# Inverse key norms written out on POOL and spread by whole transposes, and one slot more for mixed inputs, in a four-layer encoder trunk

## The chip, the core and the metric

The kernel runs on one core of a Trainium2 chip. The core has a TensorE (PE, with its weight loads shown apart as PEld), a VectorE (DVE), a ScalarE (ACT), a GpSimd (POOL) and a SyncE (SP) that issues transfers; all run their own instruction queues in order and meet through semaphores. The metric is the device time of one execution in microseconds (us), as the median of several.

## The reference

A sequence of 512 positions with 1024 channels passes two pairs of sub-layers, in fp32: a chunked spatial-gating MLP, a gated feed-forward with a short convolution, an RWKV-7 time mixer, a second such feed-forward, and a last RMS norm. The change touches the time mixer alone. What matters of it:

```
xx = token_shift(h) - h
xk = h + xx * mu[2];  xv = h + xx * mu[3]      # likewise xr, xw, xa, xg
k = xk @ w_k;  v = xv @ w_v                    # likewise r, the decay w, a, g
kk = heads(k * k_k)                            # 16 heads of 64 channels
kk = kk * rsqrt(max(sum(kk * kk, -1), 1e-24))  # a norm per position and head
k = k * (1 + (a - 1) * k_a)
y = wkv7_scan(r, exp(-exp(w)), k, v, -kk, kk * a)
```

The scan updates a 64 x 64 state per head at each position; `-kk` and `kk * a` are the two vectors of its rank-one correction.

## The kernel before

Activations are held transposed: 128 channels on the partitions, 512 positions along the free axis, in eight tiles. Every dense matmul is made of three (`mm3`, L325 to L327): high part of the weight by high part of the input, high by low, and low by high, each 128x128 by 128x512. An input tile therefore exists twice, as `mxh` and `mxl`, in a ring of ten slots for each of the two tags. `mix(i, k)` makes one: ScalarE scales the shifted tile (L669), VectorE adds the unshifted one (L670), ScalarE rounds the high part (L237), VectorE subtracts for the low part (L238).

The time mixer has three stages. First the low-rank inputs and r are projected. Then the *pairs* stage works through the eight pairs of heads (one tile of 128 channels is one pair): `decay`, `operands` and `products` make from the projected keys what the scan needs, per chunk of 64 positions, and write it to DRAM. At the same time the projections of k and v (`projections`) run as *fill*: the generator `weave` asks the fill for some steps of dense matmuls after every step of the pairs. Then the two groups of four pairs are scanned chunk by chunk, with the inversion of small triangular blocks (`invert`), the gate and the output projection beside it. The instructions are emitted in this woven order, and a scheduling layer then orders each engine's queue; the queues are in order on the chip.

In `decay`, of pair p: two matmuls (L875, L877) give decay and a, ScalarE takes their tanh, VectorE scans the decay within chunks (L887), and ScalarE makes three exponentials of it (L892, L893, L895). For the norm, ScalarE squares the scaled key (`sq`, L889), four matmuls of 2 columns (L899) sum the squares of each head, with the result turned so that positions lie on partitions: 8 numbers on each of 128 partitions (4 blocks of 128 positions, 2 heads). VectorE bounds them (L901) and takes the reciprocal (L902), `n2`. These have to be spread back over the 64 channels of each head: eight matmuls (L907), one for each block and head, whose weights are one column of `n2` repeated 64 times and whose moving operand is the identity; the result `u.q` lies in PSUM.

`operands` multiplies the scaled key by it (L926) and makes the operand tiles `ar` (L920, L921) and `bk` (L927, L928, L930, copy L933). `products` multiplies `bk` by `ar` (L949) and by a diagonal (L963) and masks the results (L953). The large scratch tile with the tag `sq` exists twice, and a pair uses it twice: for the tanh of the decay (`th`, in which the scan result lies too) and for the squares.

The keys' projection takes m = 0 to 5 one by one (each eight input tiles) and the last two together, k by k. In that last loop the values' inputs `xv` are made, up to three ahead (`k + 3`): with ten slots, eight are the keys' inputs.

## Time and profile before

| | |
|---|---|
| median of 3 runs | 1257.34 us (1256.7 to 1258.81) |
| the profiled execution, its own time | 1258.93 us |
| its span, first to last instruction | 1257.1 us |
| mean granted TensorE clock in it | 0.994 |
| busy PE / DVE / ACT / POOL | 1240.7 / 857.7 / 628.1 / 95.0 us |
| the eight groups of L907 | from 583.3 to 687.8 us |

A row of a timeline has the start and the length in us, the engine, line, operation, what is written and read, the shape, and how many instructions were merged. A group row has the busy time, then the mean length in ns, then the idle time before it and what ended that. A released wait names the engine and the line that were waited for. Matmuls are pipelined, so a row's length reaches past the start of the next; the distance of two starts is what an instruction takes of the engine. A matmul of two fp32 passes shows as two records, a transpose as one.

### The profile page before, as it was taken

To read this page: it belongs to the slowest core of one execution; us is meant where nothing else is said; L and a number is where in the kernel's file an instruction comes from. 1 tells how busy PE (TensorE), PEld (TensorE's weight loads), DVE (VectorE), ACT (ScalarE), POOL (GpSimd) and SP (SyncE) were. 2 spreads that over 40 slices of the span, in tenths; PEclk is the share of its full clock that TensorE was granted. 3 is DMA by queue.
4 is the path that set the end of the run, shared out by engine and by line. 5 is a ranking of instruction groups with operands and counts; after the bars stand their busy time and mean duration, and the time that the engine had idled before them with its cause. 6 is when DMAs were issued, how large, how long until landed. Compare 5 with 4: busy or idle time off the path is not lost.

```text
span 1257.1 us, 19429 instructions
## 1 busy us (share of the span) xinstructions
PE 1240.7 (99%) x7543; PEld 1005.7 (80%) x7543; DVE 857.7 (68%) x1413; ACT 628.1 (50%) x1081; POOL 95.0 (8%) x116
## 2 busy tenths in 40 slices
PE   9999999999999999999999999899999999999997
PEld 6878888888888888877777777678888888888886
DVE  6466568888886445675889888675677777772323
ACT  5534445555554433475677657433545444442322
POOL 4100200000000001000000013222100000000000
PEclk9999999999999999999999989999999999999999
DMA  7332357777656776325878887654323333233332
GB/s 250 113 101 84 107 174 247 246 241 248 205 172 193 225 227 195 95 92 186 216 196 230 223 270 224 224 152 135 98 88 100 101 101 90 95 97 95 107 93 80
DMA packets 125133, 201.65 MB, mean 160 GB/s; under 512 B 39856, under 2 KB 63152, under 8 KB 125040
## 3 DMA queue, kind: packets, MB, share of 16 engines
q10 hardware_dynamic: 38976, 112.87, 29.3%
q1 hardware_dynamic: 86064, 87.54, 22.4%
q8 instruction: 59, 0.97, 0.3%
q14 instruction: 34, 0.28, 0.1%
HBM read 152.93 MB, written 47.45 MB: 159 GB/s over the span
## 4 chain that ended last, share of the span: by engine, by line
PE 88%; DVE 5%; issue 1%; ACT 0%; DMA 0%; POOL 0%; ACTq 0%; DVEq 0%; POOLq 0%
PE mm L325 9%; PE mm L326 9%; PE mm L327 9%; PE aux L325 6%; PE aux L327 6%; PE aux L326 6%; PE e L325 6%; PE e L326 6%; PE us L325 6%; PE e L327 6%; PE us L326 6%; PE us L327 6%; PE aux L949 1%; DVE tt L1030 1%; PE aux L963 1%; DVE pr L1029 1%
## 5 line engine op out<-in xcount | busy, mean ns | idle before, releaser
L237 ACT CAST w<-w 128x512 fp32r<-128x512 f32 x340 | 206.1, 611 | 353.3 <-PE aux L327 91.0
L238 DVE TENSOR_TENSOR w<-w,w 128x512 fp32r<-128x512 f32 x340 | 232.2, 685 | 183.8 <-ACT w L237 183.5
L325 PE MATMUL mm<-mxh,w 128*128 128x512 f32 x408 | 166.9, 409 | 0.0
L326 PE MATMUL mm<-mxl,w 128*128 128x512 f32 x408 | 161.2, 395 | 0.9 <-DVE mxl L1167 0.9
L327 PE MATMUL mm<-mxh,w 128*128 128x512 f32 x408 | 160.8, 394 | 0.0
L352 POOL TENSOR_TENSOR ss<-ss,sq 128x512 f32<-128x512 f32 x30 | 40.7, 1358 | 769.4 <-ACT sq L350 706.7
L325 PEld LDWEIGHTS mm<-mxh,w 128*128 128x128 f32 x408 | 76.9, 189 | 19.8 <-issue 3.3
L326 PEld LDWEIGHTS mm<-mxl,w 128*128 128x128 f32 x408 | 77.0, 189 | 16.5 <-issue 1.3
L327 PEld LDWEIGHTS mm<-mxh,w 128*128 128x128 f32 x408 | 76.9, 188 | 16.5 <-issue 0.7
L554 ACT ACTIVATE cv<-z,par 128x512 f32<-128x512 f32 x88 | 71.7, 817 | 32.9 <-DVE z L552 28.0
L325 PE MATMUL aux<-mxh,w 128*128 128x512 f32 x216 | 84.5, 391 | 0.0
L325 PE MATMUL us<-mxh,w 128*128 128x512 f32 x216 | 84.5, 391 | 0.0
L327 PE MATMUL aux<-mxh,w 128*128 128x512 f32 x216 | 84.2, 390 | 0.0
L326 PE MATMUL aux<-mxl,w 128*128 128x512 f32 x216 | 84.1, 389 | 0.0
L326 PE MATMUL us<-mxl,w 128*128 128x512 f32 x216 | 84.1, 389 | 0.0
L327 PE MATMUL us<-mxh,w 128*128 128x512 f32 x216 | 84.0, 389 | 0.0
L325 PE MATMUL e<-mxh,w 128*128 128x512 f32 x208 | 81.4, 391 | 0.0
L326 PE MATMUL e<-mxl,w 128*128 128x512 f32 x208 | 81.1, 390 | 0.0
L327 PE MATMUL e<-mxh,w 128*128 128x512 f32 x208 | 80.9, 389 | 0.0
L555 DVE SCALAR_TENSOR_TENSOR cv<-z,par,cv 128x512 f32<-128x512 f32 x88 | 66.1, 752 | 19.5 <-ACT cv L554 19.5
L556 DVE SCALAR_TENSOR_TENSOR cv<-z,par,cv 128x512 f32<-128x512 f32 x88 | 66.0, 752 | 2.9
L238 DVE TENSOR_TENSOR pwl<-pw,pwh 128x512 fp32r<-128x512 f32 (+1 forms) x51 | 35.9, 704 | 19.3 <-DMA wod<-pwl 6.9
(1091 smaller groups left out, 2581.2 us busy)
## 6 DMA issues: line engine op xcount, KB each, us to landing
w<-in_wup ACTq DMA_DIRECT2D x88, 512.0 KB, 3.6
w<-in_wdn ACTq DMA_DIRECT2D x32, 512.0 KB, 3.6
st<-std SPq DMA_DIRECT2D x15, 640.0 KB, 5.2
w<-wkd ACTq DMA_DIRECT2D x16, 512.0 KB, 4.7
w<-wvd ACTq DMA_DIRECT2D x16, 512.0 KB, 5.8
w<-wod ACTq DMA_DIRECT2D x16, 512.0 KB, 4.2
w<-in_wdn ACTq DMA_DIRECT2D x16, 384.0 KB, 3.4
w<-in_wsu ACTq DMA_DIRECT2D x8, 512.0 KB, 3.7
```

Of the source, the lines that this page charges most:

```text
L237: nc.scalar.copy(hi[r, :n], src)
L238: (lo_eng or nc.vector).tensor_tensor(lo[r, :n], src, hi[r, :n].bitcast(F32), ALU.subtract)
L325: mm(acc, wh, xh, start=first, stop=False)
L326: mm(acc, wh, xl, start=False, stop=False)
L327: mm(acc, wl, xh, start=False, stop=last)
L352: nc.gpsimd.tensor_tensor(self.ss, self.ss, self.sq, ALU.add)
L554: nc.scalar.activation(c, z[:, 2:], AF.Identity, scale=cw(2, i), bias=self.p("conv_b", l * 44 + i))
L555: nc.vector.scalar_tensor_tensor(c, z[:, 1:T + 1], cw(1, i), c, ALU.mult, ALU.add)
L556: nc.vector.scalar_tensor_tensor(c, z[:, 0:T], cw(0, i), c, ALU.mult, ALU.add)
L949: nc.tensor.matmul(qs[hd][:, c - ch.start, :], bk[H[hd], c, C * hd:C * hd + P], ar[H[hd], c, :], start=True, stop=True)
L963: nc.tensor.matmul(qs[hd][:, c, :], bk[H[hd], c, C * hd:C * hd + P], dg[H[hd], c, :], start=True, stop=True)
L1029: V.tensor_tensor(q, a, b, ALU.mult)
```

## The change

In `decay`, after the reciprocal, POOL now copies the eight numbers of each partition into a tile `nb` of 8 x 64, each number 64 times. It takes a third use of the scratch tag `sq`. The eight matmuls become four transposes, each of one block's 128 x 128 part of `nb` (two heads of 64 columns). In `projections` three values' inputs are made beside the sixth key projection (m = 5), one before each of its first three steps, and the last loop keeps four ahead. For this the rings of `mxh` and `mxl` get an eleventh slot everywhere.

```
-        return self.split(self.xr, src, [P, T], "mx", bufs=10, scale=scale, lo_eng=lo_eng)
+        return self.split(self.xr, src, [P, T], "mx", bufs=11, scale=scale, lo_eng=lo_eng)
...
+            xv = []
             for m in range(KT - 2):
                 a = self.acc("mm")
-                yield from self.dense_steps(a, load.take(), r.xk)
+                for _ in self.dense_steps(a, load.take(), r.xk):
+                    if m == KT - 3 and len(xv) < 3:
+                        xv.append(r.mix(3, len(xv)))
+                    yield
                 yield from key(m, a)
                 yield
 
             ws = [load.take(), load.take(False)]
             accs = [self.acc("mm") for _ in range(2)]
-            xv = []
             for k in range(KT):
                 for j in range(2):
                     self.mm3(accs[j], self.wcols(ws[j], k * P, P), r.xk[k], k == 0, k == KT - 1)
-                while len(xv) < min(k + 3, KT):
+                while len(xv) < min(k + 4, KT):
                     xv.append(r.mix(3, len(xv)))
...
             n2 = tile_([P, 8], "n2", 2)
             V.tensor_scalar(n2, q[:, 0:8], 1e-24, None, ALU.max)
             V.reciprocal(n2, n2)
+            nb = scratch("sq").rearrange("p (b c) -> p b c", c=C)
+            G.tensor_copy(nb, bc(n2, C))
             yield
             u.q = self.acc("e")
             for b in range(4):
-                for hd in range(2):
-                    nc.tensor.matmul(u.q[H[hd], b * P:(b + 1) * P], n2[:, 2 * b + hd:2 * b + hd + 1].to_broadcast([P, C]),
-                                     self.c("ident", P), start=True, stop=True)
+                nc.tensor.transpose(u.q[:, b * P:(b + 1) * P], nb[:, 2 * b:2 * b + 2].rearrange("p h c -> p (h c)"),
+                                    self.c("ident", P))
             yield
```

The lines of the changed file are shifted: its L902 is the sum of squares (L899 before), L907 the copy, L911 the transposes, L953 the products (L949 before), L878 and L880 the decay's matmuls (L875 and L877 before). The scheduling layer orders the queues anew. TensorE's queue from the sum of squares of pair 0 on (`mm` and its three lines are dense fill), before and then changed:

```order
L899 MATMUL e_4935<-cst,sq_4927 128x2 x4
L327 MATMUL mm_4915<-mxh_4820,w_759_4864 128x512
L325 MATMUL mm_4915<-mxh_4833,w_759_4864 128x512
L326 MATMUL mm_4915<-mxl_4834,w_759_4864 128x512
L907 MATMUL e_4955<-cst,n_777_4940 64x128 x8
L327 MATMUL mm_4915<-mxh_4833,w_759_4864 128x512
```

```order
L902 MATMUL e_4935<-cst,sq_4927 128x2 x4
L327 MATMUL mm_4915<-mxh_4820,w_759_4864 128x512
L325 MATMUL mm_4915<-mxh_4833,w_759_4864 128x512
L326 MATMUL mm_4915<-mxl_4834,w_759_4864 128x512
L327 MATMUL mm_4915<-mxh_4833,w_759_4864 128x512
L325 MATMUL mm_5009<-mxh_4754,w_771_4916 128x512
L911 MATMUL e_4957<-cst,sq_4943 128x128 x4
```

Three dense matmuls stood between the sum and the spreading, now there are five. The same place of pair 5, before and then changed (`aux` and `us` are the products of an earlier pair):

```order
L899 MATMUL e_5688<-cst,sq_5680 128x2 x4
L327 MATMUL mm_5489<-mxh_4833,w_864_5373 128x512
L325 MATMUL mm_5490<-mxh_4833,w_887_5487 128x512
L326 MATMUL mm_5490<-mxl_4834,w_887_5487 128x512
L327 MATMUL mm_5490<-mxh_4833,w_887_5487 128x512
L949 MATMUL aux_5785<-ar_5577,bk_5583 128x128
L949 MATMUL us_5786<-ar_5577,bk_5583 128x128
L949 MATMUL aux_5785<-ar_5577,bk_5583 128x128
L907 MATMUL e_5737<-cst,n_939_5693 64x128 x8
```

```order
L902 MATMUL e_5685<-cst,sq_5677 128x2 x4
L953 MATMUL aux_5773<-ar_5574,bk_5580 128x128
L953 MATMUL us_5774<-ar_5574,bk_5580 128x128
L953 MATMUL aux_5773<-ar_5574,bk_5580 128x128
L953 MATMUL us_5774<-ar_5574,bk_5580 128x128
L953 MATMUL aux_5827<-ar_5574,bk_5580 128x128 x2
L911 MATMUL e_5729<-cst,sq_5693 128x128 x4
L878 MATMUL e_5791<-lr_4355,l_926_5614 128x512
```

Four dense matmuls and three products stood between, now six products and no dense matmul. In pair 1 three dense matmuls and two products become two and three, in pair 6 two dense matmuls and one product become five products; in pairs 2, 3, 4 and 7 between 7 and 15 dense matmuls stand there beside small ones. POOL's queue in this stage, which held one small fill for each pair (`gt`), now:

```order
L894 MEMSET gt_4929 128x8 [waits DVE_49]
L907 COPY sq_4943<-n_777_4940 128x512 [waits DVE_49,PE_49,Activation_49]
L894 MEMSET gt_5029 128x8 [waits DVE_49,Activation_49,Pool_49]
L907 COPY sq_5043<-n_800_5040 128x512 [waits DVE_49,PE_49,Activation_49]
L894 MEMSET gt_5157 128x8 [waits DVE_49,Activation_49,Pool_49]
```

A copy waits for VectorE (the reciprocal), PE (an earlier reader of its buffer) and ScalarE (the exponentials that read the decay from it), and the next pair's fill stands behind it.

More of the change, by code (lines that the diff above doesn't have):

```diff
@@ L190, in warm @@
     def warm(self):
-        x = self.xr.tile([P, T], mybir.dt.bfloat16, tag="mxh", bufs=10, name=self.uid("warm"))
+        x = self.xr.tile([P, T], mybir.dt.bfloat16, tag="mxh", bufs=11, name=self.uid("warm"))
         self.nc.vector.memset(x, 0.0)
@@ L334, in operand @@
     def operand(self, src, scale=None, lo_eng=None):
-        return self.split(self.xr, src, [P, T], "mx", bufs=10, scale=scale, lo_eng=lo_eng)
+        return self.split(self.xr, src, [P, T], "mx", bufs=11, scale=scale, lo_eng=lo_eng)
     def absorb(self, k, gain):
@@ L608, in output @@
         for k in range(0, KT, 2):
-            o.append(self.xr.tile([P, 2, n], F32, tag="mxh", bufs=10, name=self.uid("o")))
+            o.append(self.xr.tile([P, 2, n], F32, tag="mxh", bufs=11, name=self.uid("o")))
             for i in range(2):
@@ L795, in key @@
                 S.copy(ks[m], a)
+            xv = []
             for m in range(KT - 2):
                 a = self.acc("mm")
-                yield from self.dense_steps(a, load.take(), r.xk)
+                for _ in self.dense_steps(a, load.take(), r.xk):
+                    if m == KT - 3 and len(xv) < 3:
+                        xv.append(r.mix(3, len(xv)))
+                    yield
                 yield from key(m, a)
@@ L804, in projections @@
             accs = [self.acc("mm") for _ in range(2)]
-            xv = []
             for k in range(KT):
@@ L808, in projections @@
                     self.mm3(accs[j], self.wcols(ws[j], k * P, P), r.xk[k], k == 0, k == KT - 1)
-                while len(xv) < min(k + 3, KT):
+                while len(xv) < min(k + 4, KT):
                     xv.append(r.mix(3, len(xv)))
@@ L902, in decay @@
             V.reciprocal(n2, n2)
+            nb = scratch("sq").rearrange("p (b c) -> p b c", c=C)
+            G.tensor_copy(nb, bc(n2, C))
             yield
@@ L905, in decay @@
             for b in range(4):
-                for hd in range(2):
-                    nc.tensor.matmul(u.q[H[hd], b * P:(b + 1) * P], n2[:, 2 * b + hd:2 * b + hd + 1].to_broadcast([P, C]),
-                                     self.c("ident", P), start=True, stop=True)
+                nc.tensor.transpose(u.q[:, b * P:(b + 1) * P], nb[:, 2 * b:2 * b + 2].rearrange("p h c -> p (h c)"),
+                                    self.c("ident", P))
             yield
@@ L1163, in gate @@
             while len(outs[g]) <= i:
-                outs[g].append(tuple(self.xr.tile([P, T], F32R, tag=t, bufs=10, name=self.uid(t)) for t in ("mxh", "mxl")))
+                outs[g].append(tuple(self.xr.tile([P, T], F32R, tag=t, bufs=11, name=self.uid(t)) for t in ("mxh", "mxl")))
             oh, ol = (x[:, ts] for x in outs[g][i])
@@ L1189, in load @@
             if g == c == 0:
-                st = [t for _ in range(2) for t in (self.xr.tile([P, T], F32, tag=tag, bufs=10, name=self.uid(tag))
+                st = [t for _ in range(2) for t in (self.xr.tile([P, T], F32, tag=tag, bufs=11, name=self.uid(tag))
                                                     for tag in ("mxh", "mxl"))]
```

## The prediction

> **What bounds the kernel now.** I read the page's first and fourth parts, then busy time by stretches, then single instructions around the place that is edited.
>
> ```profile
> span 1257.1 us, 19429 instructions
> ...
> PE 1240.7 (99%) x7543; PEld 1005.7 (80%) x7543; DVE 857.7 (68%) x1413; ACT 628.1 (50%) x1081; POOL 95.0 (8%) x116
> ...
> PE 88%; DVE 5%; issue 1%; ACT 0%; DMA 0%; POOL 0%; ACTq 0%; DVEq 0%; POOLq 0%
> ```
>
> TensorE is busy 99% of the span and makes up 88% of the chain of waits. So time is lost or won where TensorE gets fewer or more matmuls, or where it stands. A busy PE can hide a stand of some tenths of a us, because ends are modelled; I therefore judge by the distance between starts.
>
> The edit lies in the stage that prepares the eight pairs of heads, about 575 to 712 us. Busy us of PE, PEld, DVE, ACT and POOL in three stretches (then granted clock, share of the DMA engines, GB/s):
>
> ```profile
> 630.00:668.00 38.00, 38.00 (x314) 29.74 (x311) 33.06 (x55) 31.57 (x58) 0.22 (x2) 1.00 0.75 207
> 668.00:712.00 44.00, 43.33 (x346) 33.67 (x345) 42.42 (x100) 24.02 (x52) 0.72 (x3) 1.00 0.88 247
> 735.00:770.00 35.00, 34.92 (x486) 26.23 (x480) 33.45 (x84) 18.70 (x43) 9.19 (x11) 1.00 0.92 288
> ```
>
> PE stands nowhere in the first, and for 0.7 us in the second, where VectorE is nearly full (42.42 of 44.00) and PE waits 0.5 us for it. POOL is all but free. A saved PE microsecond is therefore worth a microsecond here, as long as PE finds its operands ready.
>
> **The removed and the added PE work.** One pair's spreading of inverse norms before (L907, eight matmuls with 64 columns of weights), and four whole transposes of the kind that comes instead, from the later normalisation (L1307):
>
> ```profile
> 607.35 1.09 PE L907 MATMUL e<-cst,n 128*64 128x128 f32 x16
> 608.38 0.50 PE L326 MATMUL mm<-mxl,w 128*128 128x512 f32 x1
> ...
> 758.38 0.66 PE L1307 MATMUL aux<-cst,y 128*128 128x128 f32 x4
> 758.79 0.48 PE L325 MATMUL mm<-mxh,w 128*128 128x512 f32 x1
> ```
>
> From the first start to the start of the next work: 608.38 - 607.35 = 1.03 us for the old form (16 records), 758.79 - 758.38 = 0.41 us for the new (4 records). Over eight pairs 8 x (1.03 - 0.41) = 4.9 us of PE time go. This is the gain if nothing waits.
>
> **The added step and its wait.** The transposes now need the copy that POOL writes, which needs the reciprocal (L902). Pair 0 before, PE, VectorE and ScalarE:
>
> ```profile
> 581.60 0.95 PE L899 MATMUL e<-cst,sq 128*128 128x2 f32 x8
> 582.41 0.48 PE L327 MATMUL mm<-mxh,w 128*128 128x512 f32 x1
> 582.73 0.39 PE L325 MATMUL mm<-mxh,w 128*128 128x512 f32 x1
> 582.95 0.39 PE L326 MATMUL mm<-mxl,w 128*128 128x512 f32 x1
> 583.27 1.09 PE L907 MATMUL e<-cst,n 128*64 128x128 f32 x16
> ...
> 582.59 0.17 DVE L901 TENSOR_SCALAR n<-e 128x8 f32<-128x8 f32 x1 [3.15 <-PE e L899]
> 582.79 0.20 DVE L902 RECIPROCAL n<-n 128x8 f32<-128x8 f32 x1
> 582.91 0.65 DVE L920 TENSOR_TENSOR ar<-kn,gt 128x512 f32<-128x512 f32 x1
> ...
> 581.53 0.61 ACT L895 ACTIVATE rb<-sq 128x512 f32<-128x512 f32 x1
> ```
>
> Let T be the start of L899, 581.60. The reciprocal ends at 582.99, T+1.39. The copy's buffer is the third use of a double-buffered scratch and must also wait until the decay's exponential (L895) has read it, at 582.14: earlier, so not the limit here. Before, three dense matmuls cover the way to L907 at T+1.67, and a dense matmul is 0.22 to 0.23 us (582.73 to 582.95).
>
> What the copy costs stands in no row: 512 elements of each partition, one operand. The nearest POOL rows are a fill without an operand and an addition with two; beside them what POOL does to VectorE:
>
> ```profile
> L1010 POOL MEMSET tt<- 128x1024 f32 x2 | 1.9, 956 | 17.3 <-DVE li L1019 17.3
> L352 POOL TENSOR_TENSOR ss<-ss,sq 128x512 f32<-128x512 f32 x30 | 40.7, 1358 | 769.4 <-ACT sq L350 706.7 <-issue 62.5
> ...
> 798.35 1.65 POOL L1263 TENSOR_TENSOR wt<-vu,gc 64x256 f32<-64x256 f32 x2
> ...
> 798.42 1.10 DVE L1301 TENSOR_TENSOR y<-y,gr 128x512 f32<-128x512 f32 x1 [0.45 <-POOL gr L382]
> ...
> L1301 DVE TENSOR_TENSOR y<-y,gr x8: 692/836/1096, 755.3 to 856.6; 128x512 f32<-128x512 f32 x8
> ```
>
> Half of the 1024-element fill is 0.48 us, the two-operand form takes 1.36. I take 0.5, as a copy is nearer the fill (one stream fewer to read than the addition, and no arithmetic), and keep both ends. The last three rows show that the two engines hinder each other: L1301, 0.69 us alone, takes 1.10 when a POOL instruction that reads SBUF started just before it. The reverse must be expected too. L920 starts 0.08 us before the reciprocal ends, ahead of the copy, and it has both operands in SBUF; so the copy waits for the rest of it, about 0.5 us, or for nothing at the other bound. The hand-overs (DVE to POOL, POOL to PE with its weight load) I put at 0.05 and 0.15 us; between L902's end and L907 lie 0.28, and 0.04 between L899's end and L901.
>
> [...]
>
> Need and cover, pair by pair, with the order of the changed program:
>
> Pair 0: five dense matmuls now, T+1.67+2 x 0.227 = T+2.12 until PE reaches the transposes. Need T+1.39+0.05+0.5+0.5+0.15 = T+2.59. PE stands 0.47 us.
>
> Pair 1: two dense matmuls and three products (L949). Up to the last dense one T+1.13, 0.33 to the first product, 0.63 for three (next rows, 652.72 to 653.35): T+2.08. Same need, 0.5 us.
>
> Pairs 5 and 6 have the least cover:
>
> ```profile
> 650.79 0.95 PE L899 MATMUL e<-cst,sq 128*128 128x2 f32 x8
> 652.72 0.37 PE L949 MATMUL aux<-ar,bk 64*128 64x128 f32 x1
> 653.35 1.09 PE L907 MATMUL e<-cst,n 128*64 128x128 f32 x16
> ...
> 651.77 0.17 DVE L901 TENSOR_SCALAR n<-e 128x8 f32<-128x8 f32 x1
> 652.49 0.20 DVE L902 RECIPROCAL n<-n 128x8 f32<-128x8 f32 x1
> ...
> 668.10 0.95 PE L899 MATMUL e<-cst,sq 128*128 128x2 f32 x8
> 669.08 0.17 DVE L901 TENSOR_SCALAR n<-e 128x8 f32<-128x8 f32 x1
> 669.29 0.20 DVE L902 RECIPROCAL n<-n 128x8 f32<-128x8 f32 x1
> ```
>
> Pair 5: six products stand between. They run two at a time, so some 0.85 us by the 0.63 for three; the first starts at about T+0.72, a tenth before a dense matmul would (582.41 - 581.60 = 0.81): T+0.72+0.85 = T+1.57. The reciprocal ends at T+1.90 (652.69 - 650.79), as L920 stands ahead of it there too; need T+1.9+0.05+0.5+0.5+0.15 = T+3.1. PE stands 1.5 us. Pair 6: five products, T+1.42. The reciprocal ends at T+1.39 (669.49 - 668.10), and the neighbours on VectorE are 0.2 us pieces of the inversion, so no waiting for the port: need T+2.1, 0.7 us.
>
> Pairs 2, 3, 4 and 7 have 7 to 15 dense matmuls in between (1.6 to 3.4 us) and 13 to 16 or more small ones: nothing, with up to 0.5 us each if the exponentials come late. Behind a standing transpose on PE's queue stand the next decay's matmuls and the dense fill, all of which are delayed with it; POOL's queue holds only the next pair's 0.1 us fill (L891) behind the copy.
>
> Sum: -4.9 + 0.47 + 0.5 + 1.5 + 0.7 = -1.7 us.
>
> **The mixed inputs.** Eleven slots in place of ten let three of the values' inputs be made beside the sixth key projection; the rest follow one position further ahead. Each costs two VectorE steps and two on ScalarE, the same number as before:
>
> ```profile
> 632.83 0.64 DVE L238 TENSOR_TENSOR mxl<-mt,mxh 128x512 fp32r<-128x512 f32 x1
> 633.99 0.75 DVE L670 SCALAR_TENSOR_TENSOR mt<-h,omu,mt 128x512 f32<-128x512 f32 x1
> ```
>
> Three of them move 3 x (0.64 + 0.75) = 4.2 us of VectorE work some 10 us earlier, into a stretch with more room. They hide behind PE, which never waited for them (38.00 of 38.00 in 630 to 668): I book nothing. Had they no cover they would cost those 4.2 us; a gain lies only in VectorE being freer for the scans of pairs 4 and 5.
>
> The profiled execution took 1258.93 us, 1.6 above the median of the runs shown, 1257.34, and its span is 1257.1. The difference is taken over to the median: 1257.34 - 1.7 = **1255.6 us**.
>
> **Rivals.** *The cover holds*: the copy never waits for VectorE and the hand-over to PE costs 0.05 us. Pairs 0 and 1 then need T+1.99, within their cover; pair 5 stands 0.9 us and pair 6 0.6. Result -4.9 + 1.5 = -3.4, 1253.9 us. For it: POOL is idle and the copy has one operand. Against it: the stretched L1301.
>
> *The copy is as slow as the addition* (slower than before). At 1.36 us and with 0.5 us waiting, pairs 0 and 1 stand 1.35 us each, pair 5 2.35, pair 6 2.1: 7.2 us. Meanwhile VectorE's L921 is held off 0.86 us longer in each of pairs 5 to 7, 2.6 us in the stretch where it has 1.6 us to spare: 1.0 us more at PE's wait for the inversion, and 0.3 behind it for the products' operands. -4.9 + 7.2 + 1.3 = +3.6, 1260.9 us. It decides from a copy of about 0.95 us on, where the four waits reach 5 us. For it: the operand is spread out of eight numbers per partition, and all two-operand rows run at this price.
>
> *The half clock moves.* Once in the middle PE runs at half the clock:
>
> ```profile
> 724.00:728.00 4.00, 4.00 (x52) 3.57 (x45) 3.55 (x13) 2.17 (x6) 0.00 (x0) 0.50 0.49 145
> 728.00:732.00 4.00, 4.00 (x42) 2.83 (x41) 3.09 (x7) 2.36 (x6) 1.37 (x2) 0.64 0.51 107
> ```
>
> Those rows make 2.0 + 1.4 = 3.4 us lost. It follows a stretch of small matmuls whose order the change shifts. If it does not come, the forecast becomes 1255.6 - 3.4 = 1252.2 us. Against it: the small matmuls themselves stay. The opposite, a second such stretch set off by the transposes in their new place, makes 1259.0. The later normalisation's transposes were followed by none (clock 1.00 from 735 to 770 above). [...]
>
> **How the numbers follow.** What a measurement of this kernel can tell from no change is about 0.2%, 2.5 us: 1254.8 to 1259.9. Chances: the forecast 0.37 (its own range 1254.8 to 1257.5); the cover holds 0.24; no half clock 0.13; slow copy 0.23; a second half clock 0.03. Faster 0.24 + 0.13 = 0.37, same 0.37 + 0.03 = 0.40, slower 0.23. The range leaves out about a tenth on each side, half of the slow copy's cases and the faster half of the two fast ones together: 1252.2 to 1260.9.
>
> **What would show it.** Right: L907's rows give way to groups of 4 at 0.41 us; POOL has eight new rows of 0.5 to 1.0 us; PE's idle time before the transposes is largest at pairs 5 and 6, where POOL is named as releaser; L920 or L921 grows beyond 0.69 us. The first rival is right if PE names POOL hardly at all, the second if the copies exceed 0.95 us. The forecast is wrong if the order of the changed program is kept by other waits, so that PE is late itself at pairs 5 and 6; or if the waits in the scan, from 770 to 862 us, which I take as unchanged, shift by more than a microsecond.

## The result: 1269.5 us, slower, and where the time went

| | before | after |
|---|---|---|
| median of 8 runs | 1257.36 us (1256.55 to 1260.56) | 1269.47 us (1262.44 to 1377.59) |
| ratio to before, 95% interval | | 1.0071 (1.0054 to 1.0089) |
| profiled run: time, span, mean clock | 1258.93, 1257.1, 0.994 | 1262.65, 1260.9, 0.992 |

The change makes the kernel slower, by 0.7%; forecast were 1255.6 us and a range of 1252.2 to 1260.9. (One run of after, 1377.59 us at a mean clock of 0.843, is left out of the ratio.) The other seven lie on two levels that go with TensorE's granted clock: 1262.44 and 1262.65 us at 0.993 and 0.992, and 1269.27 to 1270.31 at 0.985 to 0.987. The first profile is one of the lower level.

The page of after, its first and fourth parts:

```profile
span 1260.9 us, 19251 instructions
...
PE 1241.0 (98%) x7447; PEld 1005.8 (80%) x7447; DVE 861.0 (68%) x1413; ACT 628.2 (50%) x1081; POOL 101.3 (8%) x124
...
PE 86%; DVE 5%; DMA 1%; issue 1%; ACT 1%; POOL 1%; ACTq 0%; POOLq 0%; DVEq 0%
```

TensorE has 96 records fewer (7543 before) and yet is busy 0.3 us longer. The stretches of the prediction, now (busy PE, PEld, DVE, ACT, POOL; granted clock; DMA share; GB/s):

```profile
630.00:668.00 38.00, 37.05 (x284) 29.25 (x281) 32.79 (x55) 29.73 (x55) 1.95 (x4) 0.96 0.77 215
668.00:712.00 44.00, 42.70 (x291) 33.02 (x290) 41.78 (x100) 24.92 (x55) 2.39 (x5) 1.00 0.88 243
735.00:770.00 35.00, 34.53 (x453) 25.69 (x451) 32.73 (x78) 18.57 (x40) 8.41 (x12) 1.00 0.96 295
724.00:728.00 4.00, 4.00 (x52) 3.65 (x52) 3.73 (x10) 0.53 (x1) 0.00 (x0) 0.76 0.60 181
728.00:732.00 4.00, 4.00 (x16) 3.23 (x15) 3.26 (x11) 3.04 (x7) 0.00 (x0) 0.50 0.26 79
```

In 630 to 668 TensorE, never idle before, stands for 0.95 us, and its clock is 0.96 where it was 1.00. The stands are those that were forecast. In the group row of the transposes (idle time last) and the row of POOL's copies (shortest, median, longest in ns):

```profile
L911 PE MATMUL e<-cst,sq 128*128 128x128 f32 x32 | 5.9, 313 | 2.4 <-POOL sq L907 1.4 <-POOL gt L894 0.9
...
L907 POOL COPY sq<-n x8: 611/870/1029, 582.1 to 687.1; 128x512 f32<-128x512 f32 x8
```

2.4 us in all: 0.29 at pair 0, 0.31 at pair 1, 0.95 at pair 5, 0.82 at pair 6. The new half clock lies beside them. Around the two new half-clock stretches, and in the full-clock stretch ahead of each:

```profile
603.20:606.65 3.45, 3.45 (x42) 3.30 (x42) 1.17 (x3) 2.98 (x7) 0.00 (x0) 1.00 0.79 175
606.65:610.05 3.40, 3.40 (x11) 2.60 (x11) 2.24 (x4) 2.04 (x4) 0.98 (x2) 0.50 0.83 243
...
651.00:654.43 3.43, 2.94 (x29) 2.46 (x28) 3.34 (x9) 3.30 (x8) 0.47 (x1) 1.00 1.08 338
654.43:657.84 3.41, 2.96 (x9) 2.57 (x10) 2.93 (x5) 1.40 (x3) 0.45 (x2) 0.50 0.70 207
```

In this profile the half clock comes in pieces of 3.41 us (one, one and two of them), and their starts (606.65, 654.43, and the old one at 726.11) lie 47.78 and 119.46 us apart, 14 and 35 times 3.413 us: I read a grid of windows from it, fixed through the run. TensorE was busy for the whole window before the first piece, 3.45 of 3.45 us, but with this:

```profile
L967 PE MATMUL us<-dg,bk 64*128 64x64 f32 x16 | 2.2, 278 | 0.0
L967 PE MATMUL aux<-dg,bk 64*128 64x64 f32 x16 | 2.2, 278 | 0.0
L902 PE MATMUL e<-cst,sq 128*128 128x2 f32 x8 | 1.1, 254 | 0.0
L325 PE MATMUL mm<-mxh,w 128*128 128x512 f32 x1 | 0.6, 614 | 0.0
L327 PE MATMUL mm<-mxh,w 128*128 128x512 f32 x1 | 0.4, 398 | 0.0
```

Thirty-two matmuls that move 64 columns through half of the rows, eight that move 2, and one or two dense ones at its edges. I count a record as its moving columns times its share of the 128 rows: 32 x 64 x 0.5 + 8 x 2 + 512 = 1550 at the most. The dense ones lie across the edges; with each shared out by its time in the window, 1224 are left. At full clock a dense matmul starts 0.227 us behind the one before (the median in before and after from 150 to 1235 us), so a window full of them moves 512 x 3.413 / 0.227 = 7700, an estimate.

This gave the theory to test, **C** (the clock): what decides is how few columns pass in a window; a window with few columns, called poor here, halves the clock of the next, which loses 1.7 us (half of 3.41). Against it stood **S**, the stands for POOL's copy; **T**, the transposes as such; and **R**, the order of TensorE's queue, moved by the early mixes or by the slots. C and R go together if the order is what makes windows poor.

A measure used below is the **clock-free time**: a profile's span less half the length of its half-clock stretches, in which TensorE is busy for most of the time (3.40 of 3.40 us from 606.65 on, 2.96 of 3.41 from 654.43 on). It is of the one profiled run of a kernel, and not of its median. Before it is 1257.1 - (3.41 + 6.83 + 6.09) / 2 = 1249.0 us (the first and the last of these stretches, near 21 us and at the end, are outside the stage), after 1260.9 - (3.41 + 3.41 + 6.83 + 7.71) / 2 = 1250.2.

### The profile page after: what moved, and what is told of

It reads as the page before. It is cut to its first block, busy times and chain, and to the rows that moved or that the text cites. A ratio compares the mean times of both kernels' runs of the same rounds, so it can differ in the third digit from the quotient of the medians.

```text
span 1260.9 us, 19251 instructions
## 1 busy us (share of the span) xinstructions
PE 1241.0 (98%) x7447; PEld 1005.8 (80%) x7447; DVE 861.0 (68%) x1413; ACT 628.2 (50%) x1081; POOL 101.3 (8%) x124
## 4 chain that ended last, share of the span: by engine, by line
PE 86%; DVE 5%; DMA 1%; issue 1%; ACT 1%; POOL 1%; ACTq 0%; POOLq 0%; DVEq 0%
PE mm L325 9%; PE mm L326 9%; PE mm L327 8%; PE aux L325 6%; PE aux L327 6%; PE aux L326 6%; PE e L325 6%; PE e L326 6%; PE us L325 6%; PE e L327 6%; PE us L327 6%; PE us L326 6%; PE aux L967 1%; DMA std<-lq 1%; DVE tt L1034 1%
```

## The experiments

Ahead of the later runs I also counted along the queue: the rows of TensorE's queue laid end to end, each with the mean spacing of its kind in the traces, and the columns summed in every position of a 3.41 us window. That is an estimate; how far it held is told below.

### The two halves, and the copy

`mixes` is the change without its lines on `nb` and the transposes (eleven slots, early inputs, `k + 4` stay), `spread` has these lines alone (ten slots, mixes as before). In `copy_oldmm` POOL's copy stays and the old matmuls read it; in `dvecopy` VectorE writes the copy:

```
 copy_oldmm, against after
-                nc.tensor.transpose(u.q[:, b * P:(b + 1) * P], nb[:, 2 * b:2 * b + 2].rearrange("p h c -> p (h c)"),
-                                    self.c("ident", P))
+                for hd in range(2):
+                    nc.tensor.matmul(u.q[H[hd], b * P:(b + 1) * P], nb[:, 2 * b + hd],
+                                     self.c("ident", P), start=True, stop=True)
 dvecopy, against after
-            G.tensor_copy(nb, bc(n2, C))
+            V.tensor_copy(nb, bc(n2, C))
```

> The change's other half alone: eleven slots and the earlier mixed inputs, with the eight 64-column matmuls per pair as before. Theory C (the clock): what is lost comes from 3.41 us windows in which TensorE's matmuls move too few columns (below about 1500 to 1700, a matmul counted by its moving columns times its share of the 128 rows; four such windows preceded a half-clock window in the two traces, of 1280 to 1488), and these arise because four transposes move 512 columns where sixteen matmul passes moved 2048. Then this kernel has no half-clock window before 700 us and takes 1256 to 1260.5 us, within 0.2% of before. Rival R (the order): the early mixes alone move the dense matmuls away from the products; then half-clock windows appear between 600 and 660 us here too, and it takes 1261 us or more. Rival S (the stands before the transposes): 1257.4 us, no change.

> The spreading alone: GpSimd's copy and four transposes per pair, ten slots and the mixed inputs as before. Theory C: half-clock windows of 3.41 us appear between 600 and 690 us and more of them between 710 and 735 us than before's two; each costs 1.7 us; time 1259 to 1270 us, mean clock of a run 0.986 to 0.993. Rival S: only the stands count, 4.9 us less work against some 2.4 us of standing: 1254.9 us, with the clock as before. Rival R: also 1254 to 1256 us, as the mixes are those of before.

> Everything of the change but the transposes: GpSimd's copy stays, and the eight 64-column matmuls per pair read it, as they did the reciprocal. It has the waits of the change and none of its saving on TensorE. Theory C: the matmuls' 2048 columns per pair stay in the windows, so no half-clock window before 700 us; time = before + the stands, some 2.4 us: 1259 to 1261 us. Rival S with the order (the clock follows from the stands, not from the transposes): half-clock windows between 600 and 690 us as in the change, 1264 us or more. If GpSimd's copy cost nothing it would be 1257.4 us.

> The change with the copy written by VectorE, right behind its reciprocal, in place of GpSimd. The hand-over of 0.16 us and the meeting of two engines at the memory go, and a copy of 512 elements should take 0.4 to 0.65 us in place of 0.62 to 1.03. Theory C: the transposes move as few columns as in the change, and the stands were only 2.4 us in all, so half-clock windows stay and the time is 1259 to 1269 us. Rival S: the stands shrink from 2.4 us to under 1, and the time falls to 1256 to 1258 us unless VectorE's 8 x 0.5 us more delay the inversion at 700 us.

| | median us | ratio to before, 95% | half clock in the profile, from 560 to 900 us | clock-free |
|---|---|---|---|---|
| mixes | 1273.52 | 1.0115 (1.0098 to 1.0131) | 41.0 us in 5 stretches | 1248.8 |
| spread | 1264.37 | 1.0065 (1.0040 to 1.0090) | 34.1 in 4 | 1249.4 |
| copy_oldmm | 1272.42 | 1.0109 (1.0089 to 1.0128) | 34.1 in 5 | 1249.2 |
| dvecopy | 1263.72 | 1.0068 (1.0039 to 1.0097) | 17.1 in 3 | 1248.0 |

The profiled runs took 1273.69, 1272.19, 1273.68 and 1262.27 us. `spread` and `dvecopy` also have two levels (1262.60 to 1264.68 and 1272.19 to 1273.24; 1261.64 to 1263.97 and 1270.95 to 1275.47), and the profile of `spread` is of the upper one.

The clock-free times lie within 1.0 us of before's 1249.0, while the medians lie 5.5 to 15.3 us above before's (1258.18 beside these runs): nearly all of the loss is half clock. T falls: `mixes` and `copy_oldmm` have no transpose in this place and lose most, against what I expected of both. S falls as the cause: in `mixes` nothing waits for a copy, and with VectorE's copy, 0.42 us long, the stands shrink to 0.8 us and the ratio to before stays (1.0068, the change 1.0071). R is right on `mixes`, and wrong on `spread`: each half by itself brings the half clock. `mixes`, the stretches of 709 to 743 and 780 to 794 us:

```profile
708.80:712.20 3.40, 2.24 (x44) 1.76 (x43) 3.37 (x3) 0.00 (x0) 0.00 (x0) 1.00 0.83 231
712.20:722.50 10.30, 10.30 (x88) 6.94 (x88) 2.27 (x4) 7.31 (x10) 1.12 (x2) 0.50 0.22 56
722.50:729.30 6.80, 6.80 (x123) 5.66 (x121) 5.88 (x10) 3.02 (x7) 0.00 (x0) 1.00 0.49 137
729.30:743.00 13.70, 13.70 (x115) 10.91 (x114) 5.33 (x18) 5.04 (x11) 1.23 (x2) 0.50 0.48 142
780.50:783.90 3.40, 2.11 (x60) 1.47 (x60) 3.34 (x8) 2.66 (x4) 1.31 (x2) 1.00 0.94 245
783.90:794.10 10.20, 10.20 (x156) 8.01 (x154) 5.86 (x13) 5.99 (x11) 0.64 (x3) 0.50 0.20 61
```

The half clock now lasts three and four windows at a time (10.3, 13.7 and 10.2 us). In the windows ahead, TensorE also stood for 1.2 and 1.3 us.

### More work, and another order with the same work

`filler` adds 40 matmuls to the change whose result is overwritten at once. The other three alter only the table that says how many dense steps are woven in per step of the pairs (the first number of the first group is for pairs 0 to 3, that of the second for pairs 4 to 6):

```
 filler
+        def busy(q):
+            nc.tensor.matmul(q[:, 0:256], self.c("ident", P), self.cst[:, 0:256], start=True, stop=True)
 after_r2, before_r2 and before_r22, against after and before
-RATES = ((1.9, 2), (1.9, 6, 2.2), (0.66, 2, 1.15), (0.72, 2), (2, 2), (1.2, 6, 2.2))
 after_r2 and before_r2
+RATES = ((1.9, 2), (2.0, 6, 2.2), (0.66, 2, 1.15), (0.72, 2), (2, 2), (1.2, 6, 2.2))
 before_r22
+RATES = ((2.0, 2), (2.0, 6, 2.2), (0.66, 2, 1.15), (0.72, 2), (2, 2), (1.2, 6, 2.2))
```

> The change with 40 matmuls more that nobody reads: each moves 256 columns of a constant in two passes (512 columns) into a buffer that is overwritten right after, one ahead of the sums, the transposes and the last products of each pair, and two ahead of each block of the inversion; some 0.22 us each, 9 us of TensorE work in all, of which the stands of 2.4 us at the transposes can hide a part. Theory C, as the six traces so far have it: of 19 windows of 3.41 us at full clock in which fewer than 2200 columns moved (times the share of the 128 rows) all were followed by half clock, of 1827 with more than 2900 none. The added matmuls lift nearly every window between 570 and 740 us above that. So the half-clock windows there go, the work costs up to 9 us, and the time is 1258 to 1264 us with little spread from run to run: less than the change's 1269.5, with more work. Rival: if the clock does not follow the columns moved, the time is the change's plus the work, 1275 us or more.

> The change with one number of the table of rates altered: from pair 4 to pair 6, 2.0 dense steps are woven in per step of the pairs where there were 1.9. No instruction is added or taken away; dense matmuls only come a little earlier in TensorE's queue. Counted along the queue, the low windows around pair 6 and the inversion (1224 and 1784 columns at the lowest) rise to about 2200, and the one of pair 1 and 2 at about 600 us (1406) stays. Theory C: fewer half-clock windows between 660 and 740 us, 1254 to 1264 us. Rival: if the transposes or the copy's waits make the loss, it stays at 1262 to 1270 us.

> The kernel before with the first two rates at 2.0 in place of 1.9; nothing else. Counted along the queue only one low window is left before 740 us (1807 columns), where the kernel before has four. Theory C: 1252 to 1257 us, with a mean clock of 0.997 or more, if the scan, from 770 us on, does not lack the dense work that now comes earlier; if it does, half-clock windows or waits after 770 us and 1258 us or more. Rival (the clock does not follow the order): 1257 to 1259 us, no change.

> The kernel before with the second rate alone at 2.0 in place of 1.9. Counted along the queue the low windows near 670 and 710 us go and those near 600, 615 and 645 us stay (1690 columns at the lowest, each open for a fifth of the possible positions of the window). Theory C: 1253 to 1258 us, between the kernel before and the one with both rates at 2.0. Rival: 1257 to 1259 us.

| | median us (range) | ratio to before, 95% | clocks of the runs | clock-free |
|---|---|---|---|---|
| filler | 1269.19 (1268.23 to 1271.24) | 1.0093 (1.0080 to 1.0106) | 0.994 to 0.995 | 1259.3 |
| after_r2 | 1263.90 (1261.32 to 1266.81) | 1.0049 (1.0035 to 1.0064) | 0.989 to 0.993 | 1249.6 |
| before_r22 | 1271.94 (1270.27 to 1275.05) | 1.0116 (1.0101 to 1.0131) | 0.989 to 0.993 | 1258.7 |
| before_r2 | 1258.99 (1256.16 to 1263.30) | 1.0011 (1.0000 to 1.0023) | 0.990 to 0.997 | 1247.4 |

`filler` has 9.1 us more clock-free time than the change (1259.3 against 1250.2), which is the added work, and the same median as the change's upper level: the work is paid for by the clock, whose runs no longer fall below 0.994. Three stretches of it (575 to 640, 640 to 704, 704 to 745 us):

```profile
575.00:640.00 65.00, 64.59 (x435) 50.27 (x435) 50.05 (x86) 44.30 (x83) 5.23 (x10) 1.00 0.71 197
640.00:704.00 64.00, 63.96 (x453) 49.55 (x452) 58.12 (x120) 41.76 (x81) 3.33 (x7) 1.00 0.84 230
704.00:745.00 41.00, 36.91 (x476) 28.67 (x474) 27.80 (x62) 22.60 (x41) 2.36 (x4) 0.92 0.55 157
```

No half clock is left up to 704 us; one stretch of two windows stays, at 709.8. My sum for it, 1258 to 1264, was 5 us too low: I had left out the half clock outside the stage and the 1.8 us around the span. The median of `after_r2` lies 5.6 us under the change's, with one digit of a table altered and no instruction more or less; but the intervals of the two ratios overlap, and 1263.90 lies in the range of the rival as well as in that of C, so this run decides little. `before_r22` shows the price of the other side: dense steps that come earlier are missing in the scan, where TensorE is then idle for 14.4 us between 740 and 900 where it was 5.6 (sums of its idle times), at a good clock. `before_r2` can't be told from before; C had forecast 1253 to 1258 for it.

### Slots alone, and a finer weave

`slots` is the kernel before with `bufs=11` for the mixed inputs in place of `bufs=10`, and nothing else. The `_fine` kernels weave steps of three dense matmuls in place of six:

```
-RATES = ((1.9, 2), (1.9, 6, 2.2), (0.66, 2, 1.15), (0.72, 2), (2, 2), (1.2, 6, 2.2))
+RATES = ((3.5, 2), (3.8, 6, 2.2), (0.66, 2, 1.15), (0.72, 2), (2, 2), (2.4, 6, 2.2))
-FIRST0, WAIT, STEPS = 1, 1, (2, 2, 2, 2, 2)
+FIRST0, WAIT, STEPS = 1, 1, (1, 1, 2, 2, 2)
```

> The kernel before with eleven slots for the mixed inputs in place of ten, and nothing else: no instruction more or fewer, no other order in the code; the slots' release times alone move some rows of TensorE's queue (317 lines of difference, where the early mixes make 1580). Counted along the queue the lowest windows lie near 645 and 712 us with 1468 and 1674 columns (before: 1477 and 1786 near 675 and 714). Theory C: half-clock windows near 648 and 715 to 740 us as in the run of the early mixes, 1258 to 1268 us, and a clock-free time (the span less half of its half-clock time) within 1 us of the kernel before. Rival (the mixes' own work and waits make their 14 us): 1256 to 1259 us, no change.

> The change with the dense work of this stage woven in in steps of three matmuls in place of six (twice as many steps per step of the pairs: rates 3.5, 3.8 and 2.4), so that it is spread more finely between the small matmuls. Counted along the queue one kind of low window is left before 740 us (1890 columns at the lowest, a third of the positions). Theory C: hardly a half-clock window before 740 us; with the clock-free time of 1250 us, 4.8 us at half clock outside the stage and 1.8 us around the span: 1256 to 1262 us. Rival (transposes or stands make the loss): 1262 to 1270 us as the change. More dense work is left for the scan, where it may be too much: then TensorE is busy longer after 862 us, at the same total.

> The same finer weaving with the copy on VectorE. Counted along the queue it has the fewest low windows of all orders that were counted (an eighth of a window on average at a bound of 2250 columns). The clock-free time with VectorE's copy was 1248.0 us. Theory C: 1248 + 2.4 to 4.8 + 1.8, with at most two half-clock windows: 1253 to 1258 us. Rival: 1261 to 1275 us as with the coarse weaving.

> The kernel before with the same finer weaving (rates 3.5, 3.8, 2.4, steps of three matmuls). Theory C: its half-clock windows near 724 us go, 1252 to 1257 us; the comparison with the two other fine kernels shows what the spreading is worth when the clock does not interfere (4.9 us less work, less the stands). If the finer order makes new waits: 1258 us or more with a mean clock of 0.997.

| | median us (range) | ratio to before, 95% | clocks of the runs | clock-free |
|---|---|---|---|---|
| slots | 1255.51 (1254.21 to 1257.19) | 0.9975 (0.9965 to 0.9984) | 0.996 to 0.998 | 1249.1 |
| after_fine | 1272.16 (1269.24 to 1275.63) | 1.0114 (1.0100 to 1.0129) | 0.981 to 0.989 | 1252.0 |
| dve_fine | 1265.26 (1263.71 to 1275.56) | 1.0082 (1.0051 to 1.0112) | 0.980 to 0.992 | 1251.1 |
| before_fine | 1268.77 (1267.62 to 1271.10) | 1.0092 (1.0078 to 1.0107) | 0.989 to 0.993 | 1256.3 |

The times forecast by theory C were missed in all four. `slots` beats before, by 0.25%, at the same clock-free time: its profile has no half clock in the stage at all. Before and `slots`, 704 to 745 us:

```profile
704.00:745.00 41.00, 40.47 (x540) 31.70 (x540) 33.25 (x74) 23.73 (x46) 3.94 (x7) 0.92 0.73 217
```

```profile
704.00:745.00 41.00, 38.32 (x572) 28.96 (x571) 34.44 (x78) 24.61 (x47) 4.08 (x7) 1.00 0.76 223
```

In the same 41 us `slots` starts 32 records more although TensorE stands 2.2 us longer. The count along the queue had put `slots` among the poor orders, wrongly. For `dve_fine` it was right up to 740 us (no half clock there in the profile), but the finer weave brings stands in the scan (9 to 11 us of idle time from 740 to 900 in the three, 5.6 before) and poor windows there: half clock at 764, 778 and 805 us. The count knows no stands, so it says little where there are many.

### Which piece of the mixes, and the upper level

`slots_ahead` and `slots_early` add one piece each to `slots`; `slots_dve` is `slots` with the transposes and VectorE's copy. `after_again` is the change once more.

```
 slots_ahead, against slots
-                while len(xv) < min(k + 3, KT):
+                while len(xv) < min(k + 4, KT):
 slots_early, against slots (xv = [] stands ahead of the loop)
-                yield from self.dense_steps(a, load.take(), r.xk)
+                for _ in self.dense_steps(a, load.take(), r.xk):
+                    if m == KT - 3 and len(xv) < 3:
+                        xv.append(r.mix(3, len(xv)))
+                    yield
```

> Eleven slots, and the later mixed inputs one position further ahead (k + 4 in place of k + 3), without the three beside the third last key; spreading as before. Counted along the queue it has hardly more low windows than eleven slots alone (one kind at 1681 columns near 712 us). Theory C with the early mixes as what moves the queue: 1254 to 1258 us, clock 0.996 to 0.998. If the position ahead is what does it: 1265 us or more, as the mixes together (1273.5).

> Eleven slots and the three values' inputs beside the third last key, without the position further ahead (k + 3 stays); spreading as before. Counted along the queue it has low windows near 645, 660 and 712 us (1482, 1929 and 1676 columns), as the mixes together. Theory C: half-clock windows there and a chain of them from 710 us on, 1265 to 1275 us, clock-free time 1248 to 1250 us. If the pieces only act together: 1254 to 1258 us.

> Eleven slots, the mixes as before, the spreading by transposes with the copy on VectorE. Clock-free I expect 1247.5 to 1249 us (VectorE's copy with the early mixes had 1248.0, eleven slots alone 1249.1). Counted along the queue low windows remain near 600 and 671 us (1483 and 1512 columns, each open for a third of the positions). So 1248.3 + 4.8 outside the stage + 1.8 around the span + one to four half-clock windows of 1.7 us each: 1256 to 1262 us, spread over several us from run to run. Rival (the spreading is harmless without the early mixes): 1253 to 1255 us, faster than eleven slots alone.

> The change once more, for a second profile: five of its seven timed runs lay at 1269 to 1270 us with a mean clock of 0.985 to 0.987, and its profiled run at 1262.65 with 0.992. Theory C: a run of the upper level has some 14 us more at half clock, in a chain of four more windows in the stretch with the fewest columns, 712 to 737 us, or 770 to 790 us, and the same clock-free time, 1250 us within 1 us. Rival (a wait makes the upper level): the same half-clock windows as in the first profile and an idle time of TensorE some 7 us longer.

| | median us (range) | ratio to before, 95% | clock-free |
|---|---|---|---|
| slots_ahead | 1256.11 (1253.95 to 1257.30) | 0.9984 (0.9975 to 0.9992) | 1249.5 |
| slots_early | 1269.25 (1266.57 to 1272.45) | 1.0093 (1.0078 to 1.0108) | 1250.2 |
| slots_dve | 1274.59 (1273.29 to 1275.57) | 1.0133 (1.0118 to 1.0148) | 1249.7 |
| after_again | 1269.03, one run | | 1248.0 |

So among the mixes' pieces it is the early inputs that bring the half clock; slots and position ahead do not. And the spreading brings it without them: `slots_dve` is the slowest kernel of all but has a clock-free time within 0.7 us of before. The count along the queue had made 1256 to 1262 us of it: it named poor windows near 600 and 671 us, where the profile has no half clock, and not the chain behind 710 us. `after_again` fell on the upper level. Its stretch around the chain, and `slots_dve`'s:

```profile
712.00:715.40 3.40, 2.93 (x75) 2.42 (x74) 3.40 (x4) 0.95 (x1) 0.87 (x1) 1.00 0.27 72
715.40:739.30 23.90, 23.90 (x224) 19.60 (x224) 10.67 (x26) 11.62 (x21) 0.25 (x2) 0.50 0.28 78
739.30:745.00 5.70, 5.70 (x76) 3.98 (x72) 3.30 (x7) 2.49 (x5) 1.24 (x2) 1.00 0.83 225
```

```profile
710.00:713.40 3.40, 2.96 (x55) 2.45 (x56) 3.33 (x3) 1.00 (x3) 0.00 (x0) 1.00 0.57 158
713.40:744.10 30.70, 30.70 (x297) 23.99 (x294) 11.20 (x26) 13.70 (x24) 2.35 (x4) 0.50 0.38 103
```

Seven windows in a row at half clock, and nine. The two profiles of the change differ by 17.1 us of half clock (38.4 less 21.4 in all), 8.5 us lost, and their spans by 6.4. The waits of TensorE are the same in both (transposes 2.4 us; idle from 560 to 740 us 3.4 and 3.0). So in these two profiles the upper level is this chain, as expected, and no wait. What the windows meet there are the inversion's matmuls and the last pairs' products; in `after_again`, from 712.0 to 715.4 us, ahead of the chain:

```profile
L1052 PE MATMUL aux<-ix,ti 32*32 32x32 f32 x64 | 1.4, 192 | 0.5 <-DVE ix L1023 0.5
L953 PE MATMUL aux<-ar,bk 64*128 64x128 f32 x8 | 1.2, 285 | 0.0
L327 PE MATMUL mm<-mxh,w 128*128 128x512 f32 x1 | 0.5, 512 | 0.0
L326 PE MATMUL mm<-mxl,w 128*128 128x512 f32 x1 | 0.5, 497 | 0.0
L325 PE MATMUL mm<-mxh,w 128*128 128x512 f32 x1 | 0.4, 397 | 0.0
```

### More dense work for that place

`spread_last` has the POOL copy, the transposes and eleven slots; `ahead_last` is `slots_ahead`. Their rates (the last group is for pair 7):

```
-RATES = ((1.9, 2), (1.9, 6, 2.2), (0.66, 2, 1.15), (0.72, 2), (2, 2), (1.2, 6, 2.2))
 ahead_last
+RATES = ((1.9, 2), (1.9, 6, 2.2), (0.66, 2, 1.15), (0.72, 2), (2, 2), (2.6, 6, 2.2))
 spread_last
+RATES = ((1.9, 2), (2.2, 6, 2.2), (0.66, 2, 1.15), (0.72, 2), (2, 2), (2.6, 6, 2.2))
```

> GpSimd's copy and the transposes, eleven slots, no early inputs and the position as before (k + 3), with dense rates of 2.2 for pairs 4 to 6 and 2.6 for pair 7 in place of 1.9 and 1.2. Counted along the queue no window from 695 to 745 us lies under 2700 columns, and one kind near 600 us is left at 1500. Theory C, with the stretch of 709 to 740 us as the place that decides: no chain there, at most three half-clock windows before 740 us, 1255 to 1260 us, and the upper level of 1269 us is gone; if the scan from 770 us on lacks the dense work, half-clock windows or idle time come there and it is 1260 to 1266 us. Rival (the transposes as such): 1262 to 1272 us.

> The spreading as before the change, eleven slots and the position ahead (k + 4), with a dense rate of 2.6 for pair 7. Counted along the queue no window before 745 us lies under 2130 columns. Theory C: no half-clock window before 740 us in any run, clock 0.997 to 0.998, 1253.5 to 1256 us, as eleven slots alone (1255.5) or 1 us less. If the scan lacks the dense work: 1257 us or more.

`spread_last`: 1270.22 us (1266.03 to 1279.95), ratio 1.0111 (1.0088 to 1.0135), clock-free 1258.4. `ahead_last`: 1263.50 us (1262.29 to 1263.82), 1.0039 (1.0027 to 1.0051), clock-free 1254.8. Neither profile has half clock between 610 and 860 us, so with more dense work in that place the clock stayed up there; but the scan is starved. The profile of `spread_last` is of its fastest run (1266.03, clock 0.996); its other runs lie at 0.982 to 0.993, and where their half clock falls was not seen. Its median lies above both ranges of theory C and within the rival's 1262 to 1272, so it does not speak for C. Waits of TensorE in `ahead_last`, 740 to 900 us (total, times, longest):

```profile
PE aux L1307 <- DVE y L1301: 3.4, 1, 3.4
PE us L1267 <- DVE wt L1257: 1.8, 3, 0.7
PE mm L325 <- DVE h L1151: 1.6, 1, 1.6
```

Before, the largest of these was 1.6 us in two waits, the idle time there 5.6 us in all; here it is 11.9, in `spread_last` 11.6. The dense work is one stock, and what the pairs get the scan lacks.

## Why the prediction was wrong

**The steps on the spreading held in size.** Four stands were forecast at 0.47, 0.5, 1.5 and 0.7 us, 3.2 in sum; measured were 0.29, 0.31, 0.95 and 0.82, 2.4. The spreading's own time fell by 4.8 us where 4.9 were forecast (below). Pair 0 and pair 5 of after, VectorE's, POOL's and TensorE's rows:

```profile
581.81 0.65 DVE L924 TENSOR_TENSOR ar<-kn,gt 128x512 f32<-128x512 f32 x1
582.06 0.87 POOL L907 COPY sq<-n 128x512 f32<-128x512 f32 x1 [36.90 <-DVE n L905]
582.38 1.10 DVE L925 TENSOR_TENSOR ar<-rt,gt 128x512 f32<-128x512 f32 x1
582.99 0.66 PE L911 MATMUL e<-cst,sq 128*128 128x128 f32 x4 [0.29 <-POOL sq L907]
...
653.61 0.20 DVE L905 RECIPROCAL n<-n 128x8 f32<-128x8 f32 x1
653.72 0.64 DVE L925 TENSOR_TENSOR ar<-rt,gt 128x512 f32<-128x512 f32 x1
653.96 0.86 POOL L907 COPY sq<-n 128x512 f32<-128x512 f32 x1 [16.77 <-DVE n L905]
654.88 1.12 PE L911 MATMUL e<-cst,sq 128*128 128x128 f32 x4 [0.95 <-POOL gt L894]
```

The copy was forecast at 0.5 us of waiting for the VectorE instruction that started before it and 0.5 of its own. Its row starts 0.25 us behind that instruction's and is 0.87 us long, and it splits as forecast: L924 ends at 582.46 and the copy 0.47 us later, at 582.93. In pair 5 L925 ends at 654.36 and the copy at 654.82. In seven of the eight pairs the copy ends 0.47 us behind the end of the VectorE instruction that ran when it started; in pair 3, where none ran, it took 0.61 us in all. The other way round, the VectorE instruction that starts during the copy ends 0.55 us behind it in pair 0 (L925, 1.10 us long). So the ends of the rows say that the one waits for the other. Pair 6, for which I had put no such waiting, has it too: its copy is the longest with 1.03 us, and it stands 0.82 us where 0.7 were forecast.

**A term was missing from the sum.** Counted from each start to the next, without idle time and with half-clock time taken by half, between 560 and 900 us, the spreading fell from 8.19 to 3.42 us, 4.8 as forecast (4.9). But the products (L949, now L953) rose from 20.25 to 22.29, the last products from 16.71 to 17.89 and the sums of squares from 6.75 to 7.27: 3.7 us came back in matmuls that were not touched (3.2 in `after_again`). With 2.4 us of stands that makes -4.8 + 3.7 + 2.4 = +1.3, against +1.2 between the first profiles' clock-free times. Why they take longer stays open: that small matmuls do so when they stand behind each other I only suppose, and no run isolates it. The second profile of the change, 1248.0, shows that a clock-free time itself moves by 2 us with where the half clock falls, so these two sums bear no finer reading.

**The step that failed is "I book nothing" for the mixed inputs, and with it the clock, which the sum took as unchanged in both halves.** I took it from TensorE's full 38.00 of 38.00 us that VectorE's moved work is hidden. This may hold: the clock-free times are 1248.8 in `mixes` and 1250.2 in `slots_early`, before 1249.0, and such a time moves by 2 us. But the early inputs also move dense matmuls in TensorE's queue, and this costs 11 to 15 us, nearly all by the clock (`slots_early` 1269.25, `mixes` 1273.52). The spreading alone, for which the sum had -1.7, does not gain either: `spread` lies 6.2 us above the runs of before that were taken beside it, at a clock-free time of 1249.4, and `slots_dve` 16.6 us above those beside it, at 1249.7.

**And the rival of a second half-clock stretch was mis-sized.** It had the right mechanism, a stretch of small matmuls whose order the change shifts, and the sentence against it, that the small matmuls stay, was the error: `mixes` has the same matmuls in another order, and 41.0 us of half clock from 560 to 900 us. I gave it one stretch, 3.4 us, and 0.03. The two profiles show 13.7 and 30.7 us of half clock in the stage where before had 6.8: 3.4 and 12 us more lost. I also hung it on the transposes; `mixes`, with none, loses more. And where they are, they mostly do not stand in the poor windows: in the ten profiles with transposes, 19 full-clock windows between 560 and 760 us were followed by half clock, and 17 of them hold none. So most of these windows are poor by other small matmuls that now follow each other, and not by the transposes; what in the new order does it, pair by pair, no run isolates. Whether a transpose counts like a matmul for the clock, no run here separates: with their columns left out of the count given at the end, its first two bands read 31 of 32 and 15 of 32 in place of 30 of 31 and 16 of 28, too small a difference to decide it.

**Right** were the waits of the scan, taken as unchanged (idle 740 to 900 us: 5.6 before, 5.8 after), the place of the stands, the copy's price with its waiting, and POOL's eight rows within 0.5 to 1.0 us but for one of 1.03. The rival of the slow copy forecast 1260.9 with all of the loss in waits: the lower level comes near its number for another reason.

## What to carry to other kernels

Where one engine is busy 99% of the time, as TensorE is here, an edit elsewhere can still cost through the order that it gives that engine's queue (the early inputs 11 to 15 us): before trusting "hidden", lay out the new queue and look for stretches with little dense work, above all where several kinds of small matmuls now follow each other. That is a warning sign and not a forecast: the count along the queue led to wrong times for `slots`, `slots_dve` and the finer weaves. Compare kernels by their clock-free time as well as by their medians, since one tells the work and waits and the other the windows. A rate that is tuned to one order is not tuned to the next: here eleven slots won 0.25% (0.16% with the position ahead), and every other new order lost or could not be told from before.

## What the runs showed of the hardware that was not expected

The half clock also followed windows in which TensorE was busy all the time. Over the 19 profiles whose window grid can be read off in the stage, 150 to 1235 us, I took each full-clock window and whether the next one was at half clock. A record's columns are spread evenly over the length of its row:

| columns moved in a full-clock window | windows | followed by half clock |
|---|---|---|
| under 1700 | 31 | 30 |
| 1700 to 2200 | 28 | 16 |
| 2200 to 2900 | 72 | 9 |
| over 2900 | 5778 | 0 |

With a record counted where it starts, some windows move to a neighbouring band (34 of 36, 12 of 31, 9 of 63, none of 5779), so the edges are rough. In 16 of the 55 windows ahead of half clock TensorE had no idle time between its rows; in the others it stood for up to 3.1 us, which also lets few columns pass. Idle time alone is the weaker sign: of 19 windows with more than 1 us of it but over 2900 columns none was followed by half clock, and of ten with hardly any (under 0.05 us) and under 1700 columns all were.

By the estimate above a full-clock window holds at most 7700, so in these profiles the bound lies at about a quarter of it (1700 to 2200). On the first six profiles it looked sharper (19 of 19 under 2200 in the count made then; 20 of 23 by the rule used here). Going back took more columns in these profiles: of windows already at half clock 42 of 47 with under 2400 columns were followed by another, 10 of 33 with 2400 to 3100, none of 27 above. At half clock a dense matmul starts 0.427 us behind the one before (the median of 15 such distances in before and after), so such a window holds some 4100 by the same estimate: the half clock ended after 23 of the 33 windows between 59 and 76% of that, and after all 27 above. This would account for a chain of seven windows where nearly the same queue, met by the grid at another point, passes with two: the two levels of the change. That the grid's place decides the level is not shown; two profiles are too few.

The grid lies elsewhere in the second profile of the change: the chain of `after_again` starts at 715.4 us, where the grid of the first profile has 606.65 + 32 x 3.413 = 715.87. The window from 603.20 to 606.65 us, with half clock behind it, had no idle time in its rows (3.45 of 3.45 us busy, 1224 columns); of the two signs counted here the columns moved tell such windows from others better.

Lastly, the same copy of 8 numbers to 512 takes 0.42 us on VectorE (`dvecopy`) and 0.61 to 1.03 on GpSimd, the waiting for VectorE included:

```profile
L907 DVE COPY sq<-n x8: 419/424/428, 581.7 to 681.8; 128x512 f32<-128x512 f32 x8
```
